# The end of an attention stage: places taken by halves, first output tiles half by half, weights two tiles ahead

## Chip, cores and metric

The kernel runs on one core of a Trainium2 chip. The metric is the device time of one execution in microseconds. The time before is the median of three executions, and one further execution was recorded by the profiler.

## The reference

The program is a two-layer trunk on a sequence of 1024 tokens with 1024 channels, all in float32: layer 0 is a gated linear attention with a convolutional feed-forward, layer 1 is a banded softmax attention with a convolutional feed-forward, and a final norm follows. The change lies in layer 1's attention and in the steps behind it. These are the parts that matter:

```python
CHUNK, B_HEADS, B_HEAD_DIM, LEFT_CHUNKS = 64, 16, 64, 8      # BAND = 9 * 64 keys

def rmsnorm(x, g):
    return x * lax.rsqrt(jnp.mean(x * x, axis=-1, keepdims=True) + EPS) * g

def chunk_attention(xn, w_q, rel_bias, w_out, k_pad, v_pad):
    q = (xn @ w_q).reshape(bsz, nc, CHUNK, B_HEADS, B_HEAD_DIM)...
    bias = rel_bias[:, clip(rel)]                   # one learned bias per head and distance
    def one_chunk(args):                            # 64 queries against 576 keys
        s = jnp.einsum("bqhd,bkhd->bhqk", q_n, k_band) * scale + bias
        s = jnp.where(valid, s, NEG_INF)
        p = jax.nn.softmax(s, axis=-1)
        return jnp.einsum("bhqk,bkhd->bqhd", p, v_band)
    o = lax.map(one_chunk, (jnp.arange(nc), q))
    return o.reshape(bsz, seq, B_WIDTH) @ w_out

# layer 1:
h = h + chunk_attention(rmsnorm(h, b_norm), w_q, rel_bias, w_out, k_pad, v_pad)
h = h + conv_ffn(rmsnorm(h, f_norm), ...)           # starts with xn @ w_up
```

## The kernel before

Activations lie with channels on the partitions: a matrix of 1024 channels and 1024 tokens is eight tiles of 128 channels, each in two halves of 512 tokens (`s` is the half, `k` the tile). Every float32 operand of a dense product is split into a high part (a cast on ScalarE, for activations and weights) and a low part (a subtraction on VectorE or GpSimd), and a product is three matmuls: high x high, high x low, low x high (`dense`, lines 120 to 122). One such triple on 512 columns is called a unit here.

Attention works on eight pairs of heads, `p` = 0 to 7. For each pair three tiles are projected (keys, queries, values; 16 units each, half 0 first). Beside them run the score blocks of an earlier pair: `score` (L2109 to L2125: matmuls, bias and row maximum on VectorE in one instruction, the negated maximum in a second one, exponential and row sum on ScalarE, reciprocal on VectorE, scaling on GpSimd), then transposes of the probabilities (`turn_run`, L2170), their split, and the product with the values (`apply_run`, L2215 and L2216), whose sum is written to `oT`. Finished pairs 0 to 5 are written to DRAM (`d_o`) and read back as the activations of the output projection.

The order of instructions on every engine is written by a planner (`Flow`) when the kernel is built. It keeps a planned time `T`, a cost for each engine's steps (`wv.on`), a list of short steps with ranks, and a queue of dense tiles, `wv.dense`. It takes a short step when one is due, and otherwise one unit of the dense queue. The engines then work through their instructions in that order and wait for each other's data on the chip. Of the dense tiles that follow the current one, the planner loads and splits weights ahead, with this function (`brief` is False in the kernel before):

```python
while len(self.nxt) < (2 if self.brief else 1):
    ...
    next(e[2])                                   # issues the load of the weights
    self.nxt.append([e[2], 1, self.T, e[1], 8])
if split and self.nxt and self.nxt[0][1] == 1 and (split > 1 or self.T >= self.nxt[0][2] + 6.0):
    self.nxt[0][1] = 2
    self.nxt[0][4] = next(self.nxt[0][0]) or 8   # the split; it gives the unit at which the next one may come
```

It is called from a tile's second unit on, with `split` true from the unit that the current tile has given. Where a tile's split has not come when the tile itself is due, it is put there.

The activations of the output projection lie in the places of the projection's inputs, `xh` and `xl`. They are taken (`act_tiles`) when the last value tile (pair 7) has been summed for both halves. From then on `early_o` casts the pairs 0 to 5 that were read back (L2263, low part L2266, odd tiles on GpSimd), and `own_act` the pairs 6 and 7 from `oT` (L340 and L341). `first_parts` computes the first output tiles over the six early pairs (`NO` = 6): tile 0 in both halves and tile 1 in half 0, advancing together with the pair `k` as the outer loop. `part` does tiles 2 to 7, `rest(0)` and `rest(1)` add pairs 6 and 7 of one half. `rest` also issues the steps of the norm in front of the feed-forward (`norm_steps`): squares, their sum, a matmul that sums over channels (`pss`, L372), square root, a matmul that broadcasts (`psb`, L385), product, cast and low part. Half 0 of that norm runs beside the remaining tiles of half 1, paced by `tail`; half 1 runs at the start of the feed-forward, whose first weights are `r` (L1439) and whose first matmuls are `pu` (L1393 to L1395).

Of the kernel before, what the change touches and what calls it, by code (L numbers as in the profile page):

```python
# [9 lines left out]
F32 = mybir.dt.float32  # L10
# [6 lines left out]
P = 128  # L17
# [11 lines left out]
def trunk_kernel(  # L29
# [94 lines left out]
    def hs(s):  # L124
        return slice(s * HALF, (s + 1) * HALF)
# [222 lines left out]
    env = {"acc": sum_in_acts}  # L348
    hp = wp = None

    def norm_steps(h, s, g, dst, keep=False):


        run = env["run"](s) if "run" in env else None
        acc = run if run is not None else env["acc"](s)
        before = None
        for k in range(KT):
            sq = acc if k == 0 else env["tmp"]()
            nc.scalar.activation(sq, h[k][:, hs(s)], AF.Square)
            if before is not None:  # L360
                nc.vector.tensor_tensor(acc, acc, before, op=ALU.add)
            before = sq if k > 0 else None
            yield
        if run is not None:
            acc = env["acc"](s)
            nc.vector.tensor_tensor(acc, run, before, op=ALU.add)
            yield
        else:
            nc.vector.tensor_tensor(acc, acc, before, op=ALU.add)
        pss = env["aux"]("pss")  # L370
        for t in range(4):
            mm(pss[:, 2 * t : 2 * t + 2], acc[:, t * P : (t + 1) * P], ones[:, 0:2], start=True, stop=True)  # L372
        rs = rsn[:, s]
        nc.scalar.activation(rs, pss[:, 0:8], AF.Sqrt, scale=1.0 / SEQ, bias=epst)
        nc.vector.reciprocal(rs, rs)
        yield
        act_tiles((s,), dst)

        def low(t_, k):
            eng = (nc.gpsimd if k < 4 else nc.vector) if keep and s == 1 else (nc.vector if k % 2 == 0 else nc.gpsimd)  # L380
            eng.tensor_tensor(dst[1][k][s], t_, dst[0][k][s].bitcast(F32), op=ALU.subtract)  # L381

        psb = env["aux"]("psb")
        for t in range(4):
            mm(psb[:, t * P : (t + 1) * P], rs[:, 2 * t : 2 * t + 1].broadcast_to([P, P]), ident, start=True, stop=True)  # L385
        before = None
        for k in range(KT):
            t_ = h[k][:, hs(s)] if keep else env["tmp"]()
            if g is None:
                nc.vector.tensor_tensor(t_, psb[:, 0:HALF], h[k][:, hs(s)], op=ALU.mult)  # L390
            else:
                nc.vector.scalar_tensor_tensor(t_, h[k][:, hs(s)], g[:, k : k + 1], psb[:, 0:HALF], op0=ALU.mult, op1=ALU.mult)
            nc.scalar.copy(dst[0][k][s], t_)
            if before is not None:
                low(*before)
            before = t_, k
            yield
        low(*before)
# [1554 lines left out]
    with ExitStack() as ph:  # L1953
# [37 lines left out]
        def queue_kv(p):  # L1991
# [56 lines left out]
            def post_v(s, ps):  # L2048
                if s == 0:
                    kv["v"] = [(odd if p % 2 else even).tile([P, 8, P], F32R, name="V", tag="V", bufs=2) for _ in range(2)]  # L2050
                vt = bp.tile([P, HALF], F32, name="vt", tag="vt", bufs=3)
                nc.scalar.copy(vt, ps)
                t0 = wv.on("A", 0.6)
                wv.add(0.7, "turn", lambda: t0 - wv.slack, turn(s, vt))
                if (p, s) == (7, 1):
                    act_tiles((0, 1), acts)
                    wv.mark("acts")

            if p == 0:
                pss = next(first)  # L2060
# [36 lines left out]
        def score(u, kv, a, t, bt):  # L2097

            nk = min(t, 4) + 1
            W = nk * P  # L2100
            ps = pB.tile([P, 2, HALF], F32, name="sc", tag="sc", bufs=1)
            n = 2 if nk > 4 else 1
            w = W // n
            k0 = (t - nk + 1) * P
            qs = slice(t * P, (t + 1) * P)
            kA, qA, qL = kv["k"], kv["q"], kv["ql"]
            for i in range(n):
                c = slice(k0 + i * w, k0 + (i + 1) * w)
                mm(ps[:, i, 0:w], qA[a][:, qs], kA[a][:, c], start=True, stop=False)  # L2109
                mm(ps[:, i, 0:w], qL[a][:, qs], kA[a][:, c], start=False, stop=True)  # L2110
            wv.pe(2 * n, max(0.11, w * 0.45e-3))
            S = bp.tile([P, n, w], F32, name="sS", tag="sS", bufs=6)
            st = bp.tile([P, 4], F32, name="st", tag="st", bufs=8)
            nc.vector.tensor_tensor_reduce(out=S, in0=ps[:, 0:n, 0:w], in1=bt[:, 0:W][:, ::-1].rearrange("p (n w) -> p n w", n=n), op0=ALU.add, op1=ALU.max, scale=1.0, scalar=3.0 * NEG, accum_out=st[:, 0:1])  # L2114
            nc.vector.tensor_scalar(st[:, 1:2], st[:, 0:1], -1.0, None, op0=ALU.mult)
            sc_free[0] = t0 = wv.on("D", 0.35 + 1.04e-3 * W)

            def power():
                nc.scalar.activation(S, S, AF.Exp, bias=st[:, 1:2], accum_out=st[:, 2:3])
                wv.later(wv.on("A", 0.45 + 0.75e-3 * W), share)  # L2120

            def share():
                nc.vector.reciprocal(st[:, 3:4], st[:, 2:3])  # L2123
                t_ = wv.on("D", 0.13)
                nc.gpsimd.tensor_scalar(S, S, st[:, 3:4], 1.0, op0=ALU.mult, op1=ALU.mult)  # L2125
                wv.mark(u, wv.on("G", 0.2 + 1.04e-3 * W, t_))

            wv.later(t0, power)
            return S.rearrange("p n w -> p (n w)"), t - nk + 1

# [101 lines left out]

        def close(p, a, tp, oT, t):
            if p == 7 and a == 1 and tp % 2 == 1:
                wv.add(1, ("own", tp // 2), wv.when("acts"), own_act(oT, tp // 2, 7))
            if p < 7 and (a, tp) == (1, 3):
                if p == 6:
                    for s in range(2):
                        wv.add(1, ("own", s), wv.when("acts"), own_act(oT, s, 6))
                wv.mark(("o", p), t)  # L2240
                if p < 6:
                    wv.later(t + 5.0, lambda: (nc.sync.dma_start(out=d_o[p], in_=oT), wv.mark(("d_o", p), wv.T + 4.0)))
# [15 lines left out]
        def early_o(k, s):  # L2258
            yt = bp.tile([P, HALF], F32, name="yo", tag="yo", bufs=6)
            nc.sync.dma_start(out=yt, in_=d_o[k][:, hs(s)])  # L2260
            yield wv.T + 3.0
            yield from wait("acts")
            nc.scalar.copy(acts[0][k][s], yt)  # L2263
            t = wv.on("A", 0.65)
            yield t - wv.slack
            (nc.vector if k % 2 == 0 else nc.gpsimd).tensor_tensor(acts[1][k][s], yt, acts[0][k][s].bitcast(F32), op=ALU.subtract)  # L2266
            wv.mark(("act", k, s), wv.on("D", 0.7) if k % 2 == 0 else wv.on("G", 1.4, t))
# [23 lines left out]
            wv.on("G", 2.1, wv.on("A", 0.8))  # L2291
            return wt

        def part_end(m, s, ps):
            if m not in loaded:
                loaded.add(m)
                nc.sync.dma_start(out=h[m], in_=d_h[m])
            nc.vector.tensor_tensor(h[m][:, hs(s)], ps, h[m][:, hs(s)], op=ALU.add)
            wv.on("D", 0.7)

# [2 lines left out]
        def first_parts():  # L2303
# [2 lines left out]
            wts = [part_split(raws[0])]  # L2306
            yield 20
            wts.append(part_split(raws[1]))
            jobs = [(wts[m], m, s, pacc.tile([P, HALF], F32, name="acco", tag="acc", bufs=3)) for m, s in ((0, 0), (0, 1), (1, 0))]
            for k in range(NO):  # L2310
                for n, (wt, m, s, ps) in enumerate(jobs):
                    if (k, n) != (0, 0):
                        yield there(("act", k, s), *([("begun")] if (k, n) == (NO - 1, 2) else []))
                    dense(ps, wt, 0, *acts, FULL[k : k + 1], s, first=k == 0, last=k == NO - 1)
            for wt, m, s, ps in jobs:
                part_end(m, s, ps)
            yield
            yield from part_units(wts[1], 1, 1)

# [8 lines left out]

        def part(m, halves):
            raw = part_raw(m)  # L2330
            yield
            wt = part_split(raw)
            yield 3 if len(halves) == 1 else None
            for s in halves:
                yield from part_units(wt, m, s)

# [2 lines left out]
        def rest(s):  # L2339
# [10 lines left out]
            for m in range(KT):  # L2350
# [11 lines left out]
                def then(s=s, m=m):  # L2362
                    nc.scalar.dma_start(out=quarter(d_r1, m, s), in_=h[m][:, hs(s)])
                    if m == 0:
                        its[s] = norm_steps(h, s, g_f[:, 1], normed, keep=True)
                    next(its[s])
                    wv.on("D", 0.75, wv.on("A", 0.65))
                    if m == KT - 1:
# [6 lines left out]
                yield  # L2375

        def tail(it):
            for _ in it:
                yield wv.T + 1.2

        queue_kv(0)
        wv.auto = False
# [4 lines left out]
        with tc.manual_schedule():  # L2387
# [2 lines left out]
            wv.add(1, "score", lambda: 0.0, score_run())  # L2390
            wv.add(0.8, "turns", lambda: 0.0, turn_run())
            wv.add(0.6, "apply", lambda: 0.0, apply_run())
            for n, (k, s) in enumerate([(k, s) for k in range(NO) for s in range(2)]):
                wv.add(0.9, ("early", n % 6), wv.when(("d_o", k)), early_o(k, s))
            wv.add(0, "begin", wv.when(("o", 6), ("act", 6, 0), ("act", 6, 1)), begin())
            wv.dense.append((lambda: True, there(("act", 0, 0)), first_parts()))
# [104 lines left out]
```

## Time and profile before

| what | us |
|---|---|
| median of three runs | 2595.81 |
| lowest and highest of them | 2591.06, 2598.98 |
| the profiled execution, its own time | 2593.14 |
| its span in the profile | 2591.4 |
| first and last score block on VectorE (start) | 1371.0, 1822.9 |
| first matmul of the output projection (start) | 1782.2 |
| first matmul of the layer's feed-forward (start) | 1910.2 |

Times inside the profile count from the start of the span. PE is TensorE's matmul, PEld its weight load, DVE is VectorE, ACT ScalarE, POOL GpSimd, and SP the queue that issues most loads. In a row of the timeline stand start, length, engine, line, operation, what it writes from what it reads, the shape, the count, and in brackets the idle time in front of it and what ended it.

### The profile page before, as it was taken

Reading aid. Unit: us, or ns where it says so; the run is one execution under the profiler, and the core shown is the slowest. Engines: PE = TensorE matmul, PEld = TensorE weight load, DVE = VectorE, ACT = ScalarE, POOL = GpSimd, SP = SyncE. Lnnn points to the kernel's source line nnn. Section 1 sums busy time; section 2 is a strip of 40 time slices with the busy share of each in tenths; the row PEclk is TensorE's granted clock in tenths of the full one; section 3 lists DMA queues with packets and bytes.
Section 4 is the critical chain, followed back from the end, with each engine's and each line's share of the span. In section 5 each row is a group of like instructions: output and inputs, shape, how many; then the busy total and the mean of one; then the engine's idle time right before and its main releaser. Section 6 shows DMA issues by size and latency. Waiting matters only on the chain. (4 is left out here: it accounts for less than half of the span.)

```text
span 2591.4 us, 39359 instructions
## 1 busy us (share of the span) xinstructions
PE 2513.5 (97%) x13933; PEld 2078.2 (80%) x13933; DVE 1856.7 (72%) x3102; ACT 1410.0 (54%) x2708; POOL 1494.1 (58%) x1517
## 2 busy tenths in 40 slices
PE   7999999999999999999999999999999999999998
PEld 5878888888777888888778888887876788888877
DVE  5765775454588888888876666666478788888875
ACT  6444555464455656565455556655345556565543
POOL 3655554345447777777735444444443777777771
PEclk9999999999999999999999999999999999999999
DMA  4534345455336777777841111212332577777785
GB/s 128 138 99 121 116 117 164 134 178 169 96 85 143 146 148 154 153 145 153 186 145 48 47 52 57 73 37 73 133 104 78 134 150 143 154 154 153 154 194 175
DMA packets 317061, 325.93 MB, mean 126 GB/s; under 512 B 32832, under 2 KB 240960, under 8 KB 316864
## 3 DMA queue, kind: packets, MB, share of 16 engines
q1 hardware_dynamic: 285728, 219.33, 28.6%
q0 software_dynamic: 26240, 95.43, 20.6%
q10 hardware_dynamic: 4896, 8.65, 0.9%
q8 instruction: 110, 1.80, 0.3%
q14 instruction: 87, 0.71, 0.1%
HBM read 180.68 MB, written 142.67 MB: 125 GB/s over the span
## 5 line engine op out<-in xcount | busy, mean ns | idle before, releaser
L1360 POOL TENSOR_TENSOR ul<-r,uh 128x512 fp32r<-128x512 f32 x282 | 445.6, 1599 | 295.2 <-ACT uh L1381 273.9
L120 PE MATMUL acc<-xh,whi 128*128 128x512 f32 x896 | 375.5, 420 | 0.3 <-ACT xh L1099 0.2
L105 POOL TENSOR_TENSOR wlo<-wraw,whi 128x256 fp32r<-128x256 f32 (+3 forms) x338 | 248.8, 767 | 206.0 <-ACT whi L103 178.1
L122 PE MATMUL acc<-xh,wlo 128*128 128x512 f32 x896 | 353.3, 394 | 4.2 <-POOL wlo L105 4.2
L121 PE MATMUL acc<-xl,whi 128*128 128x512 f32 x896 | 353.4, 394 | 1.3 <-DVE xl L1100 0.8
L1381 ACT CAST uh<-r 128x512 fp32r<-128x512 f32 x296 | 181.7, 623 | 219.8 <-DVE r L1360 175.2
L1395 PE MATMUL pu<-xh,ul 128*128 128x512 f32 x552 | 217.3, 394 | 3.3 <-POOL ul L1360 3.2
L1393 PE MATMUL pu<-xh,uh 128*128 128x512 f32 x552 | 216.7, 393 | 2.9 <-ACT uh L1381 1.4
L1394 PE MATMUL pu<-xl,uh 128*128 128x512 f32 x552 | 216.3, 392 | 1.0 <-POOL xl L381 1.0
L2125 POOL TENSOR_SCALAR sS<-sS,st 128x640 f32<-128x640 f32 (+4 forms) x128 | 86.4, 680 | 206.5 <-DVE st L2123 197.6
L122 PEld LDWEIGHTS acc<-xh,wlo 128*128 128x128 f32 x896 | 168.8, 188 | 42.6 <-POOL wlo L105 5.3
L1714 ACT COPY stage<-pd 128x1024 f32<-128x1024 f32 x180 | 174.8, 1013 | 49.4 <-PE pd L1395 49.4
L121 PEld LDWEIGHTS acc<-xl,whi 128*128 128x128 f32 x896 | 170.0, 190 | 27.8 <-DVE xl L1100 3.1
L120 PEld LDWEIGHTS acc<-xh,whi 128*128 128x128 f32 x896 | 169.7, 189 | 24.5 <-ACT xh L1099 1.2
L1488 DVE SCALAR_TENSOR_TENSOR val<-vpre,colt,val 128x1023 f32<-128x1023 f32 (+2 forms) x92 | 153.6, 1670 | 38.6 <-ACT val L1485 38.4
L2114 DVE CUSTOM_DVE_ANT_0 sS<-sc,bt 128x640 f32<-128x640 f32 (+4 forms) x128 | 84.1, 657 | 132.5 <-PE sc L2110 87.1
L1360 POOL TENSOR_TENSOR dl<-a,dh 128x512 fp32r<-128x512 f32 x90 | 154.8, 1720 | 38.4 <-ACT dh L1381 38.4
L1488 DVE SCALAR_TENSOR_TENSOR gate<-gpre,colt,gate 128x1023 f32<-128x1023 f32 (+2 forms) x92 | 175.4, 1906 | 0.8
L1360 DVE TENSOR_TENSOR r<-r,r 128x512 f32<-128x512 f32 x168 | 131.6, 783 | 31.1 <-POOL ul L1360 29.7
L1395 PEld LDWEIGHTS pu<-xh,ul 128*128 128x128 f32 x552 | 104.3, 189 | 28.0 <-POOL ul L1360 6.6
L1393 PEld LDWEIGHTS pu<-xh,uh 128*128 128x128 f32 x552 | 104.3, 189 | 25.3 <-ACT uh L1381 1.8
L2183 ACT CAST pTh<-ptp 128x512 fp32r<-128x512 f32 (+2 forms) x176 | 75.4, 452 | 89.7 <-PE ptp L2170 86.3
(390 smaller groups left out, 7125.9 us busy)
## 6 DMA issues: line engine op xcount, KB each, us to landing
r<-in_f_w_up_dram SPq DMA_DIRECT2D x172, 256.0 KB, 4.2
d_r<-stage POOLq DMA_DIRECT2D x78, 512.0 KB, 7.9
d_c<-stage POOLq DMA_DIRECT2D x70, 512.0 KB, 7.9
a<-in_f_w_down_dram SPq DMA_DIRECT2D x72, 256.0 KB, 2.8
wraw<-in_a_w_in_dram SPq DMA_DIRECT2D x32, 512.0 KB, 4.7
d_e<-stage POOLq DMA_DIRECT2D x32, 512.0 KB, 9.1
wraw<-in_a_w_out_dram SPq DMA_DIRECT2D x16, 512.0 KB, 4.3
d_r<-h ACTq DMA_DIRECT2D x32, 256.0 KB, 3.6
```

Source lines behind the costliest of these rows:

```text
L105: nc.gpsimd.tensor_tensor(lo[:, c], raw[:, c], hi[:, c].bitcast(F32), op=ALU.subtract)
L120: mm(ps, hi[:, kw, wcol : wcol + P], rh[k][s], start=st, stop=False)
L121: mm(ps, hi[:, kw, wcol : wcol + P], rl[k][s], start=False, stop=False)
L122: mm(ps, lo[:, kw, wcol : wcol + P], rh[k][s], start=False, stop=sp)
L1360: tt = lambda eng, o, a, b, op: eng.tensor_tensor(o, a, b, op=op)
L1381: copy(hi, src)
L1393: mm(ps, w[0][:, cw], x[0], start=first, stop=False, skip_group_check=True)
L1394: mm(ps, w[0][:, cw], x[1], start=False, stop=False, skip_group_check=True)
L1395: mm(ps, w[1][:, cw], x[0], start=False, stop=last, skip_group_check=True)
L1488: nc.vector.scalar_tensor_tensor(t_[:, a:c1], p_[:, a - step : c1 - step], w[:, 2 - step : 3 - step], t_[:, a:c1], op0=ALU.mult, op1=ALU.add)
L1714: nc.scalar.copy(t_, ps)
L2125: nc.gpsimd.tensor_scalar(S, S, st[:, 3:4], 1.0, op0=ALU.mult, op1=ALU.mult)
```

## The change

The places of the output projection's activations are taken one half at a time, each when the last value tile has been summed for that half. The steps that read pairs 0 to 5 back are listed with all of half 0 first. `first_parts` runs three pairs of tile 0 in half 0, then tile 1 and tile 0 in half 0 in turn, and then tile 0 in half 1; the sums of half 0 are added to `h` at the third unit of half 1. From there on two tiles are loaded ahead (`brief`), and each tile gives an earlier unit for the next one's split. `h[m]` is loaded beside a tile's weights, if its place exists by then. The norm's last sum of squares becomes a step of its own in half 0, with new distances between the steps in `tail`. Scores are kept negated: the instruction on VectorE that adds the bias multiplies by -1 and takes the minimum, the exponential multiplies by -1, and the instruction that negated the maximum is gone; the planner's cost of a block falls from 0.35 to 0.2 plus the same part per column.

```diff
@@ norm_steps
-    def norm_steps(h, s, g, dst, keep=False):
+    def norm_steps(h, s, g, dst, keep=False, gap=False):
...
             nc.vector.tensor_tensor(acc, acc, before, op=ALU.add)
+            if gap:
+                yield
         pss = env["aux"]("pss")
@@ post_v
-                if (p, s) == (7, 1):
-                    act_tiles((0, 1), acts)
-                    wv.mark("acts")
+                if p == 7:
+                    act_tiles((s,), acts)
+                    wv.mark(("acts", s))
@@ score
-            nc.vector.tensor_tensor_reduce(..., op0=ALU.add, op1=ALU.max, scale=1.0, scalar=3.0 * NEG, accum_out=st[:, 0:1])
-            nc.vector.tensor_scalar(st[:, 1:2], st[:, 0:1], -1.0, None, op0=ALU.mult)
-            sc_free[0] = t0 = wv.on("D", 0.35 + 1.04e-3 * W)
+            nc.vector.tensor_tensor_reduce(..., op0=ALU.add, op1=ALU.min, scale=-1.0, scalar=-3.0 * NEG, accum_out=st[:, 0:1])
+            sc_free[0] = t0 = wv.on("D", 0.2 + 1.04e-3 * W)
...
-                nc.scalar.activation(S, S, AF.Exp, bias=st[:, 1:2], accum_out=st[:, 2:3])
+                nc.scalar.activation(S, S, AF.Exp, scale=-1.0, bias=st[:, 0:1], accum_out=st[:, 2:3])
@@ close and early_o: wait for ("acts", half) in place of "acts"
...
@@ part_end
+        def load_h(m):
+            if h and m not in loaded:
                 loaded.add(m)
                 nc.sync.dma_start(out=h[m], in_=d_h[m])
+
+        def part_end(m, s, ps):
+            load_h(m)
             nc.vector.tensor_tensor(h[m][:, hs(s)], ps, h[m][:, hs(s)], op=ALU.add)
@@ first_parts
             wts.append(part_split(raws[1]))
-            jobs = [(wts[m], m, s, pacc.tile(...)) for m, s in ((0, 0), (0, 1), (1, 0))]
-            for k in range(NO):
-                for n, (wt, m, s, ps) in enumerate(jobs):
-                    if (k, n) != (0, 0):
-                        yield there(("act", k, s), *([("begun")] if (k, n) == (NO - 1, 2) else []))
-                    dense(ps, wt, 0, *acts, FULL[k : k + 1], s, first=k == 0, last=k == NO - 1)
-            for wt, m, s, ps in jobs:
-                part_end(m, s, ps)
+            wv.brief = True
+            order = [(0, 0, k) for k in range(3)]
+            for k in range(3, NO):
+                order += [(1, 0, k - 3), (0, 0, k)]
+            order += [(1, 0, k) for k in range(NO - 3, NO)] + [(0, 1, k) for k in range(NO)]
+            banks, done = {}, []
+            for n, (m, s, k) in enumerate(order):
+                if n > 0:
+                    yield there(("act", k, s), *(["begun"] if (m, s, k) == (0, 1, 2) else []))
+                if (m, s, k) == (0, 1, 2):
+                    for i in range(2):
+                        part_end(i, 0, banks[i, 0])
+                if k == 0:
+                    banks[m, s] = pacc.tile([P, HALF], F32, name="acco", tag="acc", bufs=3)
+                dense(banks[m, s], wts[m], 0, *acts, FULL[k : k + 1], s, first=k == 0, last=k == NO - 1)
+            part_end(0, 1, banks[0, 1])
@@ part
             raw = part_raw(m)
+            load_h(m)
             yield
             wt = part_split(raw)
-            yield 3 if len(halves) == 1 else None
+            yield 1 if len(halves) == 1 else 3
@@ rest and tail
-                        its[s] = norm_steps(h, s, g_f[:, 1], normed, keep=True)
+                        its[s] = norm_steps(h, s, g_f[:, 1], normed, keep=True, gap=s == 0)
...
-            for _ in it:
-                yield wv.T + 1.2
+            for n, _ in enumerate(it):
+                yield wv.T + (0.8, 2.2)[n] if n < 2 else wv.T + 1.1
@@ the list of steps
-            for n, (k, s) in enumerate([(k, s) for k in range(NO) for s in range(2)]):
+            for n, (s, k) in enumerate([(s, k) for s in range(2) for k in range(NO)]):
                 wv.add(0.9, ("early", n % 6), wv.when(("d_o", k)), early_o(k, s))
```

More of the change, by code (lines that the diff above doesn't have):

```diff
@@ L2113, in score @@
             st = bp.tile([P, 4], F32, name="st", tag="st", bufs=8)
-            nc.vector.tensor_tensor_reduce(out=S, in0=ps[:, 0:n, 0:w], in1=bt[:, 0:W][:, ::-1].rearrange("p (n w) -> p n w", n=n), op0=ALU.add, op1=ALU.max, scale=1.0, scalar=3.0 * NEG, accum_out=st[:, 0:1])
-            nc.vector.tensor_scalar(st[:, 1:2], st[:, 0:1], -1.0, None, op0=ALU.mult)
-            sc_free[0] = t0 = wv.on("D", 0.35 + 1.04e-3 * W)
+            nc.vector.tensor_tensor_reduce(out=S, in0=ps[:, 0:n, 0:w], in1=bt[:, 0:W][:, ::-1].rearrange("p (n w) -> p n w", n=n), op0=ALU.add, op1=ALU.min, scale=-1.0, scalar=-3.0 * NEG, accum_out=st[:, 0:1])
+            sc_free[0] = t0 = wv.on("D", 0.2 + 1.04e-3 * W)
             def power():
-                nc.scalar.activation(S, S, AF.Exp, bias=st[:, 1:2], accum_out=st[:, 2:3])
+                nc.scalar.activation(S, S, AF.Exp, scale=-1.0, bias=st[:, 0:1], accum_out=st[:, 2:3])
                 wv.later(wv.on("A", 0.45 + 0.75e-3 * W), share)
@@ L2234, in close @@
             if p == 7 and a == 1 and tp % 2 == 1:
-                wv.add(1, ("own", tp // 2), wv.when("acts"), own_act(oT, tp // 2, 7))
+                wv.add(1, ("own", tp // 2), wv.when(("acts", tp // 2)), own_act(oT, tp // 2, 7))
             if p < 7 and (a, tp) == (1, 3):
@@ L2238, in close @@
                     for s in range(2):
-                        wv.add(1, ("own", s), wv.when("acts"), own_act(oT, s, 6))
+                        wv.add(1, ("own", s), wv.when(("acts", s)), own_act(oT, s, 6))
                 wv.mark(("o", p), t)
@@ L2261, in early_o @@
             yield wv.T + 3.0
-            yield from wait("acts")
+            yield from wait(("acts", s))
             nc.scalar.copy(acts[0][k][s], yt)
@@ L2292, in part_split @@
             return wt
-        def part_end(m, s, ps):
-            if m not in loaded:
+        def load_h(m):
+            if h and m not in loaded:
                 loaded.add(m)
                 nc.sync.dma_start(out=h[m], in_=d_h[m])
+        def part_end(m, s, ps):
+            load_h(m)
             nc.vector.tensor_tensor(h[m][:, hs(s)], ps, h[m][:, hs(s)], op=ALU.add)
@@ L2308, in first_parts @@
             wts.append(part_split(raws[1]))
-            jobs = [(wts[m], m, s, pacc.tile([P, HALF], F32, name="acco", tag="acc", bufs=3)) for m, s in ((0, 0), (0, 1), (1, 0))]
-            for k in range(NO):
-                for n, (wt, m, s, ps) in enumerate(jobs):
-                    if (k, n) != (0, 0):
-                        yield there(("act", k, s), *([("begun")] if (k, n) == (NO - 1, 2) else []))
-                    dense(ps, wt, 0, *acts, FULL[k : k + 1], s, first=k == 0, last=k == NO - 1)
-            for wt, m, s, ps in jobs:
-                part_end(m, s, ps)
+            wv.brief = True
[14 more added lines that the diff above has]
+            part_end(0, 1, banks[0, 1])
             yield
```

## The prediction, written before the result was known

> **What bounds the kernel now.** I read the page first, then the windows around the changed lines, then the list of TensorE's waits in them, then each engine's timeline at the places of the longest waits.
>
> ```profile
> span 2591.4 us, 39359 instructions
> PE 2513.5 (97%) x13933; PEld 2078.2 (80%) x13933; DVE 1856.7 (72%) x3102; ACT 1410.0 (54%) x2708; POOL 1494.1 (58%) x1517
> ```
>
> TensorE is the bound nearly everywhere. So an edit pays only where TensorE waits or where its clock is below full speed. The windows show where that is (columns: stretch, length, busy time of PE, PEld, DVE, ACT, POOL, then granted clock, DMA share, GB/s).
>
> ```profile
> 1370.00:1780.00 410.00, 408.04 (x2384) 355.74 (x2385) 261.63 (x793) 240.29 (x569) 193.45 (x320) 1.00 0.18 51
> 1780.00:1804.00 24.00, 19.33 (x77) 14.92 (x75) 12.78 (x37) 14.27 (x35) 14.74 (x15) 0.79 0.51 165
> 1788.00:1792.00 4.00, 4.00 (x13) 3.29 (x12) 2.43 (x8) 1.73 (x4) 2.82 (x4) 0.50 0.88 277
> 1895.00:1904.00 9.00, 7.13 (x23) 4.91 (x22) 4.78 (x7) 3.50 (x5) 6.73 (x5) 0.81 0.19 71
> 1904.00:1916.00 12.00, 11.85 (x53) 9.44 (x51) 11.69 (x15) 6.20 (x11) 8.12 (x7) 1.00 0.83 268
> ```
>
> The 410 us of attention proper (heads, projections) hold 2 us without TensorE work, at clock 1.00. Nothing is to be had there. The loss is in the handover to the output projection, 1780 to 1804, and again at 1895 to 1904. Busy time hides the second half of it: at 1788 to 1792 TensorE is busy 4.00 of 4.00 at half clock. The clock costs 24.00 x 0.21 = 5.04 us in the first place and 9.00 x 0.19 = 1.71 us in the second. To that come TensorE's waits from 1780 to 1932 (total, times, longest):
>
> ```profile
> PE acco L120 <- ACT whi L103: 5.3, 4, 2.7
> PE acco L121 <- POOL xl L2266: 1.9, 2, 1.6
> PE acco L122 <- POOL wlo L105: 1.3, 2, 0.7
> PE pss L372 <- DVE nacc L369: 1.3, 2, 0.9
> PE acco L120 <- DVE h L2298: 1.0, 2, 0.8
> ```
>
> All the room is therefore 5.04 + 1.71 + 5.3 + 1.9 + 1.3 + 1.0 + 0.9 (the first of the two pss waits; the other is in the next half, which the change leaves as it is) = 17.15 us, 0.66% of the run. No reading of this change gains more, unless the plan of the 410 us changes too.
>
> **First output tiles half by half, places taken by halves.** What happens there now:
>
> ```profile
> 1766.43 0.58 ACT L2052 COPY vt<-acc 128x512 f32<-128x512 f32 x1 [1.98 <-PE acc L122]
> ...
> 1778.19 0.59 ACT L2052 COPY vt<-acc 128x512 f32<-128x512 f32 x1 [0.86 <-PE acc L122]
> ...
> 1780.08 3.21 ACT L2263 CAST xh<-yo 128x512 fp32r<-128x512 f32 x6
> ...
> 1785.72 0.84 ACT L103 CAST whi<-wraw 128x768 fp32r<-128x768 f32 x1
> ```
>
> ```profile
> 1786.61 0.79 PE L120 MATMUL acco<-xh,whi 128*128 128x512 f32 x1 [2.73 <-ACT whi L103]
> 1798.44 0.50 PE L121 MATMUL acco<-xl,whi 128*128 128x512 f32 x1 [1.64 <-POOL xl L2266]
> ```
>
> ```profile
> 1794.98 2.18 POOL L2125 TENSOR_SCALAR sS<-sS,st 128x384 f32<-128x384 f32 x2 [2.96 <-DVE st L2123]
> 1797.13 2.50 POOL L2266 TENSOR_TENSOR xl<-yo,xh 128x512 fp32r<-128x512 f32 x2
> ```
>
> The last projection ends for half 0 at 1766.4 and for half 1 at 1778.2 (the two vt copies). Places are taken only after the second, so twelve casts and twelve subtractions come at once, and ACT reaches the weights of tile 1 (1785.72) behind six casts of 3.21 us. TensorE waits 2.73 us, and later 1.64 + 0.3 for the low parts on GpSimd. With places by halves the six casts of half 0 and their subtractions can run from 1766.4, beside 12 us of projection matmuls. The first tiles then start on ready data. They need nothing of half 1 for 12 units (three matmuls each; rows 1910.21 and 1910.89 below give 0.68 us), so 8.2 us plus the attention work between them. In that time GpSimd must do three subtractions at 1.25 (3.8 us), and tile 1's weights are wanted only from the fourth unit, 2 us in. Because half 0 is already marked, nothing holds the first unit back, so the split of tile 1 is put into ACT's queue ahead of the casts of half 1; that is the point where I choose. Room: 2.73 + 1.9 of waits and 5.04 of clock, 9.7. I leave 1.0 for a short wait at tile 1 and its clock: **gain 8.7**, ends 0 and 9.7.
>
> The clock part rests on the clock falling because of these waits. The trace has 0.50 right behind a wait of 2.73, a fall behind 1.64, and 1.00 through the 410 us without such a wait. The Trainium skill, "TensorE: Matmul & The Clock Gate", section "Part 1: The HAM clock gate", has the array go to half clock after an idle window of about 3.4 us. By that rule neither wait is long enough, and the 5.04 us would not go with the waits; here the row decides, and what is left if it doesn't is a rival below.
>
> What the earlier casts cost: they go into ACT's queue ahead of exponentials (L2119) and casts of probabilities (L2183), six at once, 3.21 us, for which transposes and the probability-value matmuls wait. The nearest row is in the same stretch, the only wait that TensorE has there regularly:
>
> ```profile
> PE pvt L2033 <- ACT vt L2052: 1.4, 7, 0.2
> ```
>
> Ends: nothing (the projection's eight units of half 1, 5.4 us, cover 3.21) and 3.21 plus as much clock as in the 1780 window, about 3.5 (5.04/4.63 of it), so 6.7. A gain is excluded, since there is no wait to remove. I take a **loss of 0.5**, near the pvt row, because the projection units cover it; without them it is 3.21. The DMAs of half 1 (L2260) move too; each waits on SP for a low part to free its buffer. SP's row now:
>
> ```profile
> 1782.42 4.31 SPq L2260 DMA_DIRECT2D yo<-d_o  x4
> ```
>
> Behind it on SP stand the weights of tiles 2 and 3. They are needed some 18 units later, so nothing is charged.
>
> The sums of the first two tiles of half 0 are now added four matmul units before their banks are wanted, and h is loaded when the weights are, not at the add. That removes the 1.0 of the h row: **gain 1.0**. DVE's long wait for a late h (below) goes with it; it has cost TensorE 0.2 of that 1.0.
>
> ```profile
> 1865.52 0.69 DVE L2298 TENSOR_TENSOR h<-acco,h 128x512 f32<-128x512 f32 x1 [5.53 <-DMA h<-d_h]
> ```
>
> **Weights two tiles ahead.** The planner puts a tile's split no sooner than 6 us of planned time after its load. A one-half tile is only 4.1 us long, so with one tile ahead the split came at the tile's own start:
>
> ```profile
> 1849.57 0.37 ACT L2221 COPY tm<-poT 64x256 f32<-64x256 f32 x1 [5.91 <-PE poT L2216]
> 1849.84 0.83 ACT L103 CAST whi<-wraw 128x768 fp32r<-128x768 f32 x1
> ```
>
> ```profile
> 1850.73 0.50 PE L120 MATMUL acco<-xh,whi 128*128 128x512 f32 x1 [1.19 <-ACT whi L103]
> ...
> 1880.40 1.05 PE L372 MATMUL pss<-ones,nacc 128*128 128x2 f32 x8 [0.90 <-DVE nacc L369]
> ...
> 1895.85 0.50 PE L120 MATMUL acco<-xh,whi 128*128 128x512 f32 x1 [0.53 <-ACT whi L103]
> ...
> 1898.89 0.79 PE L122 MATMUL acco<-xh,wlo 128*128 128x512 f32 x1 [0.72 <-POOL wlo L105]
> ```
>
> The cast stood behind a copy that waited for attention's last matmul. Two ahead, it can come a tile earlier. The whi waits without the first are 5.3 - 2.73 = 2.6; I take **2.3**, ends 0 and 2.6. The wait of the norm's sum (0.90) goes when the add has its own step 0.8 us ahead: **gain 0.9**; what is late next there is the square root's chain, which already lies under matmuls.
>
> The last stage of the projection (1895.85 on) has 1.3 for wlo and 1.71 of clock, 3.0. Here I expect most to come back. Its end is met by the next layer's first weights:
>
> ```profile
> 1902.78 0.37 SPq L1439 DMA_DIRECT2D r<-in_f_w_up_dram  x1
> ...
> 1906.91 1.08 POOL L1381 CAST uh<-r 128x512 fp32r<-128x512 f32 x1
> 1908.07 1.81 POOL L1360 TENSOR_TENSOR ul<-r,uh 128x512 fp32r<-128x512 f32 x1
> ...
> 1910.21 0.39 PE L1393 MATMUL pu<-xh,uh 128*128 128x512 f32 x1
> ...
> 1910.89 0.39 PE L1393 MATMUL pu<-xh,uh 128*128 128x512 f32 x1
> ```
>
> The low part ul is ready at 1909.88 and is used with the third matmul, 1910.67: 0.8 us of slack. The load follows the first tile of this stage, so the 1.3 of wlo pulls it along, the clock does not. VectorE, busy 11.69 of 12.00 at 1904 to 1916 (fourth stretch above), won't go faster either, and the next norm sum stands at its end. **Gain 1.0**, ends 0 and 3.0.
>
> **Negated scores.** One instruction less per score block:
>
> ```profile
> L2115 DVE TENSOR_SCALAR st<-st x128: 153/154/157, 1371.4 to 1823.7; 128x1 f32<-128x1 f32 x128
> ```
>
> 128 x 0.154 = 19.7 us of VectorE, which is busy 261.63 of 410: off the path. Min in place of max and a factor of -1 are taken at the same 0.75 us; no row shows them. The planner's cost per block falls by 0.15, as does the real one, so order and chip move together. Value 0; ends: a gain of 1.4 (the pvt row), a loss of 1.4 if each such wait doubles.
>
> **Sum.** 8.7 - 0.5 + 1.0 + 2.3 + 0.9 + 1.0 = 13.4 us. The profiled run took 2593.14 (span 2591.4 and 1.74 around it), so 2579.7; the median 2595.81 lies 2.67 above that run, so **2582.4**. With the ends for the unknown costs the gain runs from 9 to 17: 2578.8 to 2586.8.
>
> **Rivals.** (A) The bursts only move: six casts in attention's stream cost 3.21 and clock (6.7 in all in place of 0.5). For: ACT runs its queue in order, and the row at 1780.08 shows that six go out together. Against: projection units are in reserve. Gain 7.2: 2588.6. Half the weights' gain lost beside it gives 2590.
>
> (B) The clock is low there for another reason and stays: 4.5 of the 8.7 is lost, gain 8.9, 2586.9. Against: it falls only behind waits. The rule of the Trainium skill's page on TensorE, cited above, points this way.
>
> (C) The change doesn't do what it says: casts of both halves still come together, for instance if the buffers of half 1's loads or the weights of tile 1 still come last, and the first tiles keep their 9.7. Gain 13.4 - 8.2 = 5.2: 2590.6.
>
> (D) Slower: the new cost of a score block shifts the written order of TensorE in all seven repeated head pairs, and a score or transpose is placed ahead of what it needs. Price: one wait like that of 1786.61 with its clock, 2.73 + 2.97 = 5.7 us per pair, 40 for seven, so 2595.8 + 40 - 13.4 = 2622. It decides from three such pairs (17 against 13.4); four are needed for 0.3%. For: TensorE waits 0.2 at the same place in each of seven pairs, so the order is tight. Against: the real block shortens by what the plan's does, and VectorE has a third of its time free.
>
> **How the numbers follow.** Main case 0.60, A 0.21, B 0.04, C 0.07, D 0.08. What a measurement of this kernel can tell from no change is about 0.3%, 7.8 us: below 2588.0 is faster, above 2603.6 slower. Faster: nearly all of the main case, a quarter of A, two thirds of B: 0.66. Slower: most of D: 0.07. Same: 0.27. The range goes from 2576 (all the room and 3 us of the runs' own spread, 2591 to 2599) to 2595, which takes in A, B and C and leaves out D and little else. The likeliest case alone: 2579 to 2587.
>
> **What would show it.** Right: the 1780 window at clock near 1.00, no whi wait of over 1 us at the first tiles, casts of half 0 between 1766 and 1778, no pss wait in half 0, and a new wait of one or two us at the first pu matmuls or the second pss. Wrong: a clock below 0.9 at the handover, TensorE waits on ptp, pTh or sc between 1766 and 1800, or a wait that returns with each head pair before 1766, which would be D.

## The result and the profile after

The changed kernel takes 2579.11 us (median of six), the kernel before 2595.15 beside it: ratio 0.9941, 95% interval 0.9929 to 0.9953, 16.0 us faster. A second measurement with five rounds gave 2579.72 against 2591.07, ratio 0.9952 (0.9938 to 0.9965), 11.4 us. The forecast was 13.4 us, a ratio of 0.9948.

Times of whole runs scatter by some us even for one kernel. The two profiled executions of the changed kernel (2574.87 and 2579.72) differ ahead of the attention: its first copy starts at 1373.49 in one and at 1378.75 in the other, and up to there 5.2 and 10.2 us went to the clock (length times one minus the granted clock, over windows of 4 us). So I compare stretches inside the profiles: from the first pair's value copy (half 0, L2052, L2054 after) to the last pair's, called attention, and from there to the first feed-forward matmul that reads the low part `ul`, called handover. Before they are 390.7 and 144.2 us, after 389.4 and 130.8: 14.7 us less together. The second profile of the changed kernel gave 389.4 and 130.8 again, so this measure repeats to 0.1.

The two copies that bound attention, in the timeline of ScalarE of the changed kernel:

```profile
1373.49 0.59 ACT L2054 COPY vt<-acc 128x512 f32<-128x512 f32 x1 [0.80 <-ACT sS L2120]
...
1762.91 0.59 ACT L2054 COPY vt<-acc 128x512 f32<-128x512 f32 x1 [0.28 <-PE acc L122]
```

The windows of the changed kernel (columns as before the change):

```profile
1766.00:1780.00 14.00, 12.09 (x69) 10.15 (x68) 8.59 (x19) 10.76 (x25) 11.58 (x16) 1.00 0.46 142
1780.00:1804.00 24.00, 23.11 (x129) 19.47 (x128) 15.81 (x44) 11.98 (x32) 10.05 (x13) 1.00 0.32 109
1850.00:1895.00 45.00, 41.65 (x187) 33.40 (x187) 32.16 (x46) 21.48 (x34) 28.08 (x30) 1.00 0.54 171
```

The clock is 1.00 all through; before, 5.04 and 1.71 us went to it (6.8 over the whole handover, in finer windows). TensorE's waits from 1766 to 1920 in the changed kernel:

```profile
PE acco L122 <- POOL wlo L105: 2.7, 3, 1.9
PE pu L1395 <- POOL uh L1383: 1.4, 1, 1.4
PE pu L1397 <- POOL ul L1362: 1.1, 1, 1.1
PE pu L1396 <- POOL xl L383: 1.0, 2, 0.7
PE sc L2111 <- DVE st L2116: 0.8, 1, 0.8
```

No wait for whi, for the low parts of the projection's activations, for h or for the first half's norm sum is left. New are 1.9 at the first output tiles, 1.4 + 1.1 at the first feed-forward matmuls and 0.8 for a score block at 1789. The 1.0 for `xl` is not new: the kernel before has the same wait (L1394 for L381, 1.0 in two times), which the prediction's list leaves out. In the handover the listed waits fall from 10.6 to 6.0 us and the clock's loss from 6.8 to nothing, 11.4 of its 13.4; the other 2.0 are not resolved. How the wait of 1.9 comes about, on GpSimd and on ScalarE:

```profile
1768.42 2.44 POOL L105 TENSOR_TENSOR wlo<-wraw,whi 128x128 fp32r<-128x128 f32 x4 [11.94 <-issue]
1770.85 0.36 POOL L2126 TENSOR_SCALAR sS<-sS,st 128x128 f32<-128x128 f32 x1
1771.19 3.79 POOL L2267 TENSOR_TENSOR xl<-yo,xh 128x512 fp32r<-128x512 f32 x3
1774.97 1.43 POOL L2126 TENSOR_SCALAR sS<-sS,st 128x256 f32<-128x256 f32 x1
1776.37 2.71 POOL L105 TENSOR_TENSOR wlo<-wraw,whi 128x128 fp32r<-128x128 f32 x4
```

```profile
1764.31 3.23 ACT L2264 CAST xh<-yo 128x512 fp32r<-128x512 f32 x6
1767.43 0.84 ACT L103 CAST whi<-wraw 128x768 fp32r<-128x768 f32 x1
...
1772.53 0.84 ACT L103 CAST whi<-wraw 128x768 fp32r<-128x768 f32 x1
1773.27 1.66 ACT L2264 CAST xh<-yo 128x512 fp32r<-128x512 f32 x3
```

The high part of tile 1's weights does stand ahead of the casts of half 1 (1772.53 against 1773.27). But its low part (1776.37) stands on GpSimd behind tile 0's low part and the three subtractions of half 0.

### The profile page after: what moved, and what is told of

It reads as the page before. It is cut to its first block, busy times and chain, and to the rows that moved or that the text cites. A ratio compares the mean times of both kernels' runs of the same rounds, so it can differ in the third digit from the quotient of the medians.

```text
span 2572.9 us, 39308 instructions
## 1 busy us (share of the span) xinstructions
PE 2499.4 (97%) x13933; PEld 2071.4 (81%) x13933; DVE 1841.5 (72%) x2974; ACT 1407.6 (55%) x2708; POOL 1498.7 (58%) x1517
## 5 line engine op out<-in xcount | busy, mean ns | idle before, releaser
L1396 PEld LDWEIGHTS pu<-xl,uh 128*128 128x128 f32 x552 | 103.9, 188 | 23.4 <-POOL xl L383 2.1
```

Source lines behind the costliest of these rows:

```text
L1396: mm(ps, w[0][:, cw], x[1], start=False, stop=False, skip_group_check=True)
```

## Experiments

Stretches in us; ratio and interval against the kernel before in the same measurement, where there were five rounds. Two columns split the handover: `waits` is the sum of TensorE's listed waits in it, `clock` what it loses to a granted clock below 1.00 (length times one minus the clock, over windows of 2 us).

| kernel | attention | handover | waits | clock | sum | ratio |
|---|---|---|---|---|---|---|
| before | 390.7 | 144.2 | 10.6 | 6.8 | 534.9 | |
| after | 389.4 | 130.8 | 6.0 | 0 | 520.2 | 0.9941 (0.9929 to 0.9953) |
| e1 scores only | 389.4 | 140.5 | 11.9 | 1.7 | 529.9 | 0.9995 (0.9986 to 1.0004) |
| e2 all but scores | 390.7 | 130.9 | 4.7 | 0 | 521.6 | 0.9960 (0.9946 to 0.9973) |
| e3 halves only | 390.7 | 133.9 | 4.7 | 1.7 | 524.6 | 0.9967 (0.9956 to 0.9978) |
| e4 not two ahead | 389.4 | 132.3 | 7.2 | 0 | 521.7 | 0.9959 (0.9947 to 0.9971) |
| e5 places together | 389.3 | 130.8 | 5.8 | 0 | 520.2 | 0.9956 (0.9942 to 0.9969) |
| e6 no gap | 389.4 | 131.3 | 6.1 | 0 | 520.7 | one run |
| e7 plan's cost only | 389.4 | 140.4 | 11.8 | 1.7 | 529.8 | one run |
| e8 chip's part only | 389.7 | 142.0 | 11.1 | 3.4 | 531.7 | one run |
| e9 places only | 390.7 | 140.1 | 9.5 | 3.4 | 530.8 | one run |
| e10 after again | 389.4 | 130.8 | 6.0 | 0 | 520.2 | 0.9952 (0.9938 to 0.9965) |
| e11 six first | 389.4 | 128.6 | 4.1 | 0 | 518.0 | 0.9943 (0.9930 to 0.9955) |
| e12 six first, cast on ScalarE | 389.4 | 130.2 | 5.7 | 0.5 | 519.6 | 0.9956 (0.9943 to 0.9968) |

**Scores alone (e1), and all but the scores (e2).** e1 is the kernel before with the `score` hunks of the change, e2 the changed kernel with them taken back.

> The kernel before with the negated scores alone (instruction, exponential and the planner's cost of 0.2). Theory, that the handover's waits and clock make 11 to 12 of the 16 us and the shorter score block only tightens the written order of the head pairs: 2 to 4 us faster than before (ratio 0.9985 to 0.9992), the stretch 1780 to 1804 still with a clock below 0.85 and a wait of over 2 us for whi. Rival, that the 19.7 us which VectorE no longer works carry the gain: 8 us or more faster (ratio 0.997 or less).

> The changed kernel with the scores as before (two instructions, planner's cost 0.35). Theory: 12 to 14 us faster than before (ratio 0.9946 to 0.9954), clock at the handover 1.00, the head pairs 56.8 us apart as before instead of 56.4. Rival, that the scores carry the gain: 8 us faster at most.

The scores alone give 5.0 us inside the profile, more than the 2 to 4 expected, and their whole-run ratio can't be told from 1. Added to the rest they give 1.4 (521.6 to 520.2); e2 itself is 13.3 under the kernel before, in its band. Of e1's 5.0, 3.7 lie in the handover. It waits no less there than the kernel before (11.9 against 10.6), but loses 1.7 us to the clock instead of 6.8; the clock of 0.93 at 1780 to 1804 and a longest wait for whi of 1.2 are not the signs that the theory named. The changed kernel loses nothing to the clock in the handover, with these scores or without (e2). So the scores don't carry the gain, and of the freed 19.7 us of VectorE at most 1.4 is in it.

**The first tiles by halves alone (e3).**

```diff
 (the changed kernel, with)
-            wv.brief = True
-            load_h(m)                                  # in part
-            yield 1 if len(halves) == 1 else 3
+            yield 3 if len(halves) == 1 else None
 (scores and norm steps as before)
```

> The kernel before with the places taken by halves, the steps that read pairs back listed by halves, and the first tiles half by half; one tile ahead, splits at the old units, h loaded at the add, norm sum and scores as before. Theory: 8 to 10 us faster than before (ratio 0.9961 to 0.9969): handover at clock 1.00 with one wait of about 2 us, while the waits for whi at the later tiles (1.19, 0.85, 0.53) and for the norm's sum (0.90) stay. Rival, that the weights two tiles ahead are what frees the handover: 3 us faster or less, and a whi wait of over 2 us at the first tiles.

10.3 us less than before, a little over the band, without two tiles ahead: 5.9 of waits and 5.1 of clock, less 0.7 elsewhere. The wait of about 2 us that I expected at the first tiles isn't there (0.42 for wlo). TensorE's longest waits show that the first tiles are free and the later ones stay, and behind the wait for the norm's sum the clock fell once (1.7 us):

```profile
PE acco L122 <- POOL wlo L105: 1.9, 4, 0.7
PE acco L120 <- ACT whi L103: 1.4, 2, 0.8
PE pss L374 <- DVE nacc L369: 0.9, 1, 0.9
```

**One tile ahead (e4).** The changed kernel without `brief` and with the old split units.

> The changed kernel with one tile ahead and the old units for the splits; everything else as changed. Theory: 2 to 3 us slower than the changed kernel, so 13 to 14 us faster than before (ratio 0.9946 to 0.9950), with the waits for whi at later tiles back. Rival, that two tiles ahead carry the gain: within 8 us of the kernel before.

1.5 us more than the changed kernel: one whi wait of 1.2 is back. That is less than the 2 to 3 expected, and no more than a fraction of the gain.

**Places together (e5) and places only (e9).**

```diff
 (e5: the changed kernel, with)
-                if p == 7:
-                    act_tiles((s,), acts)
-                    wv.mark(("acts", s))
+                if (p, s) == (7, 1):
+                    act_tiles((0, 1), acts)
+                    for i in range(2):
+                        wv.mark(("acts", i))
```

e9 is the kernel before with the opposite edit: places and marks by halves, the order of steps and first tiles as before.

> The changed kernel with the places of both halves taken together, after the last projection; order of steps and tiles by halves as changed. Theory, that the early places are what lets the casts of half 0 run beside the last projection: 5 to 9 us slower than the changed kernel (ratio to before 0.996 to 0.9975), all casts behind 1770, a wait of 2 us or more at the first output tiles and mostly a clock below 0.9 behind it. Rival, that the order by halves is enough: within 2 us of the changed kernel, clock 1.00.

> The kernel before with the places taken by halves and nothing else; the steps that read pairs back are listed pair by pair and the first tiles advance in both halves together, as before. From the last value tile's half 0 (its copy on ScalarE) to the first feed-forward matmul the kernel before takes 143.8 us, the changed one 129.0. Theory after the run with both places taken together, that the order of the first tiles by halves is what counts: 139 to 145 us, with the wait for the first tiles' weights or low parts still above 1.5 us. Rival, the prediction's own step, that the early places are what frees the handover: 135 or less.

This felled the step that I thought carried the gain. With the places taken together the sum is 520.2, the changed kernel's to 0.1, although the casts of half 0 come only after the last projection:

```profile
1778.75 3.23 ACT L2265 CAST xh<-yo 128x512 fp32r<-128x512 f32 x6
```

The planner then puts attention work into the time of the casts, and the first output unit starts 7.3 us later, counted from the first copy; that work has to be done somewhere. The equal sum is made of unequal parts, though. e5 doesn't have the wait of 1.9 for tile 1's low part, and has others in its place (0.9 for `xl`, 0.6 for `oT`). Early places with the old order take 139.6 us by the measure of the expectation, in the theory's band, and give 4.1 us. Long waits stay (whi 2.6, low part 2.1):

```profile
PE acco L120 <- ACT whi L103: 4.0, 3, 2.6
PE acco L121 <- POOL xl L2266: 2.1, 1, 2.1
```

Of the 4.1, 3.4 is clock. That much less clock was lost in e8 too, which takes the places as before, so it can't be credited to the places; the waits fell by 1.1, from 10.6 to 9.5. So the order by halves frees the handover: with it, and the places late, the waits are 5.8 and the clock's loss nothing. None of the nine profiles with that order has a fall of the clock at the first output tiles; each of the five without it has one or two. Early places are worth about 1 us of waits without it, and nothing in the order of the changed kernel. What they are worth in e11's order, where the wait of 1.9 is gone, was not tried. Nor was the order in which pairs are read back tried apart from the order of the first tiles.

**Norm sum in one step with its add (e6).** `gap` off and all steps 1.2 apart.

> The changed kernel without the norm sum's own step and with 1.2 between all steps of the norm. From the first score matmul to the first feed-forward matmul the changed kernel takes 523.7 us. Theory: 0.5 to 1.5 us longer, with a wait for the norm's sum of about 0.9 in half 0. Rival: no longer, since the first feed-forward weights end the stage anyway.

525.6 from the first score to the first feed-forward matmul, 1.9 more and above the band, but the waits at that matmul (2.5) are gone in exchange; counted to the low part's matmul it is 0.5. The theory's wait returned (0.70 for the sum), and with it two for whi that it hadn't named (0.82 and 0.54). The rival is right on most of the time: the feed-forward's weights end the stage.

**Plan or chip (e7, e8).** e7 changes only `0.35` to `0.2`; e8 has the new instructions and keeps 0.35.

> The kernel before with the planner's cost of a score block at 0.2 in place of 0.35 and nothing else. From the first score matmul to the first feed-forward matmul the kernel before takes 539.7 us, and with the negated scores and this cost together 534.7. Theory, that the written order makes those 5 us: 533 to 537, pairs 56.4 us apart. Rival, that the shorter block on VectorE makes them: 539 or more.

> The kernel before with the negated scores and the planner's cost left at 0.35, so the order on every engine stays as written. Theory, that the order makes the 5 us: 538.5 to 540.5 us from the first score matmul to the first feed-forward matmul, pairs 56.8 apart. Rival, that the shorter block makes them: 537 or less, and shorter pairs.

e7 took 534.6 and does what e1 does, so the plan is enough. But e8 took 536.5, below its band: attention got 1.0 shorter without any change of order, nearly as much as with the new plan (1.3), and both together give 1.3. So either loosens the pairs, and neither theory is right alone. The instruction itself costs the same in both forms; its rows in the kernel before and in the changed one:

```profile
L2114 DVE CUSTOM_DVE_ANT_0 sS<-sc,bt x128: 291/753/827, 1371.0 to 1822.9; 128x640 f32<-128x640 f32 x64, 128x128 f32<-128x128 f32 x16, 128x256 f32<-128x256 f32 x16, 128x384 f32<-128x384 f32 x16
```

```profile
L2116 DVE CUSTOM_DVE_ANT_0 sS<-sc,bt x128: 272/754/827, 1368.8 to 1815.1; 128x640 f32<-128x640 f32 x64, 128x128 f32<-128x128 f32 x16, 128x256 f32<-128x256 f32 x16, 128x384 f32<-128x384 f32 x16
```

The other 2.2 us of e8 lie in the handover, where its waits are as long as before (whi 5.5 in all, xl 2.6), but 3.4 us go to the clock instead of 6.8. Nothing in e8 orders the handover differently, so half of that loss of the kernel before doesn't follow from its order and its waits alone; the last section shows on what else it depends.

**The changed kernel again, and two versions that go on (e10, e11, e12).** e11 and e12:

```diff
-            order = [(0, 0, k) for k in range(3)]
-            ...
+            order = [(m, 0, k) for m in range(2) for k in range(NO)] + [(0, 1, k) for k in range(NO)]
 (e12 also)
-            ... nc.gpsimd.tensor_copy if r == 0 else nc.scalar.copy)
+            ... nc.gpsimd.tensor_copy if r == 0 and (layer, c) != (1, 0) else nc.scalar.copy)
```

> The changed kernel once more, for a second profile and for times beside the next two. Theory: the same waits within 0.2 us at the same places (129 to 131 us of handover), while the clock behind them need not fall the same. Rival, that the clock follows the length of the waits: 1.00 everywhere again.

> The changed kernel with all six pairs of tile 0 in half 0 ahead of tile 1, so that the low part of tile 1's weights, which now comes 1.91 us late behind three subtractions on GpSimd, has three units (2 us) and the attention work among them more. Theory: that wait gone and 1.5 to 2 us faster than the changed kernel. Rival, that the wait only goes on to the next late thing (scores, half 1's low parts): within 0.7 us.

> As the run before, and the high part of layer 1's first feed-forward weights is cast on ScalarE (0.6 us there) instead of GpSimd (1.1 to 1.2, behind a subtraction of 1.6). Theory: the waits at the first feed-forward matmuls fall from 1.4 + 1.1 to 1.5 to 2 in all, 0.5 to 1 us faster than with six first alone. Rival: the low part still ends it on GpSimd and nothing is gained.

e10 doesn't decide between its two expectations in the handover: 130.8 us, the same waits, and the clock at 1.00 again. Ahead of the attention the same kernel lost 10.2 us to the clock where its first profile lost 5.2.

e11 is 2.2 us shorter in the profile than the changed kernel, a little more than expected, and the wait of 1.9 is gone; its median, 2575.72, is the lowest of all, 4.0 under e10 beside it, though the intervals overlap. It is the version to keep. e12 lost 1.6 of that again, which neither of its expectations had: in ScalarE's queue the cast stands behind the norm's squares, so the wait for it grew from 1.4 to 3.3.

```profile
1891.67 0.50 PE L1395 MATMUL pu<-xh,uh 128*128 128x512 f32 x1 [1.40 <-POOL uh L1383]
1893.53 0.50 PE L1397 MATMUL pu<-xh,ul 128*128 128x512 f32 x1 [1.12 <-POOL ul L1362]
```

```profile
1898.67 0.50 PE L1395 MATMUL pu<-xh,uh 128*128 128x512 f32 x1 [3.30 <-ACT uh L1383]
1900.23 0.80 PE L1397 MATMUL pu<-xh,ul 128*128 128x512 f32 x1 [0.82 <-POOL ul L1362]
```

(Above e11, below e12.)

## Why the prediction held, step by step

**The room and where it lies** held in the main: of the room of 17.15 us, the clock's 6.8 went and 4.6 of the waits. The handover as a whole gave 13.4, and attention, where I saw nothing to be had, gave 1.3.

**First tiles: 8.7 + 1.0 for h - 0.5 for the burst, 9.2 in all; e3 measured 10.3**, clock included (e3 leaves the h loads at the add). The size was right, the reason half wrong. I put it on casts that run beside the last projection; e5 shows that these are not needed. What counts is that the first units ask for half 0 only, so half as many casts and subtractions stand in front of them. That half as many stand there is read from the queues, not tried by itself. The burst that I charged with 0.5 cost at most 0.3, a wait for `ptp` in e2 and e3 that the kernel before lacks.

**The clock**: I priced it in proportion to the waits (2.97 for 2.73). It doesn't come so: each fall took 1.7 us or twice that, and e4, with nearly the waits of the changed kernel, had one just behind the stretch that I measure. The whole 6.8 went because the waits that are left didn't set off a fall, and the last section shows that this was partly luck.

**Tile 1's weights**: I argued from ScalarE's queue and was right there, but didn't follow the same tile's low part through GpSimd's queue. It waited 1.91, where I had left 1.0 with the clock; e11 took the wait away and got 2.2. In e2 and e3, with the scores as before, the same matmul waits 0.42, so the wait needs the order written for the new scores as well.

**Two tiles ahead**: 2.3 forecast, 1.5 measured (e4). **Norm sum**: 0.9 forecast, 0.5 (e6), since what is late next is the feed-forward's weights, not the square root.

**The last stage of the projection** was mis-sized: forecast a gain of 1.0 with ends 0 and 3.0, measured a loss of 0.9. From its first matmul to the low part's first use it took 1895.85 to 1910.67, 14.8 us; after it takes 15.8:

```profile
1877.99 0.39 PE L120 MATMUL acco<-xh,whi 128*128 128x512 f32 x1
...
1891.88 0.50 PE L1395 MATMUL pu<-xh,uh 128*128 128x512 f32 x1 [1.41 <-POOL uh L1383]
...
1893.74 0.50 PE L1397 MATMUL pu<-xh,ul 128*128 128x512 f32 x1 [1.12 <-POOL ul L1362]
```

The mechanism was the one named, the next layer's first weights, with a new wait of the size that I gave as its sign. What I missed is that the work of the norm's first half is not shortened by a faster projection and now falls into this stage: a subtraction for it, which itself waits 3.30 us for ScalarE, holds GpSimd until the weights' cast can start.

```profile
1889.09 1.63 POOL L383 TENSOR_TENSOR xl<-h,xh 128x512 fp32r<-128x512 f32 x1 [3.30 <-ACT xh L395]
1890.65 1.17 POOL L1383 CAST uh<-r 128x512 fp32r<-128x512 f32 x1
```

VectorE was as full as I took it to be: 11.69 of 12.00 us before (1904 to 1916), and after:

```profile
1884.00:1896.00 12.00, 9.46 (x41) 7.22 (x40) 11.69 (x17) 6.21 (x11) 8.23 (x7) 1.00 0.80 246
```

**Scores**: 0 forecast with ends of 1.4 either way; 1.4 measured, at the end.

**The sum**: 14.7 us in the stretches against the 13.4 forecast is partly luck. The first tiles and the scores gave 2.5 more than forecast; the last stage, two tiles ahead and the norm's sum gave 3.1 less. The parts as measured add up to 12.8 only, since each was tried against a different kernel.

**The rivals.** A (the bursts only move) and C (no effect at the first tiles) are out by the clock of 1.00 and by e3. One sign that I gave for being wrong did show, a wait of 0.77 on `sc` at 1789.12; e2 and e3 don't have it, so it belongs to the new scores. B (the clock stays low for another reason) is out as a whole, but it had a grain: e8 keeps the waits and loses half as much clock. D (slower through the plan in each pair) is out: the plan's shift makes attention shorter (390.7 to 389.4).

## What to carry to other kernels

When a stage begins with many small preparations, let the first products ask for half of the data first; taking the places earlier may add little. Follow a moved tile through every queue that prepares it, not only the first: the longest new wait came from the second. When a stage is shortened, look for work of other engines that is not shortened with it, and charge it at the stage's end.

## What the runs showed of the hardware

The clock's fall is not fixed by the wait in front of it. The changed kernel waited 1.91 at the first tiles and 1.4 + 1.1 at the feed-forward with the clock at 1.00 after all of them. In the handovers of all these profiles each fall goes to 0.50 and lasts 3.4 us or twice that, so it costs 1.7 us or 3.4. The falls of the kernel before in the handover:

```profile
1785.89:1792.72 6.83, 6.11 (x17) 5.05 (x18) 3.15 (x9) 4.55 (x9) 4.20 (x6) 0.50 0.83 261
1799.55:1802.96 3.41, 3.27 (x10) 2.68 (x11) 0.00 (x0) 0.04 (x1) 3.33 (x4) 0.50 0.01 2
1898.53:1901.94 3.41, 3.05 (x7) 2.47 (x8) 0.69 (x1) 1.18 (x2) 3.08 (x4) 0.50 0.19 73
```

Their starts lie on a grid: 13.66 and 112.64 us behind the first, 4 and 33 steps of 3.413. All nine falls of that execution from 311.3 to 2526.6 fit the same grid to 0.1 us (read in windows of 0.1 us). That suggests that it counts how much of a step TensorE is idle, and a wait can lie in one step or be cut in two. e4 and e10 have the same waits at the feed-forward, 1.4 and 1.1, at nearly the same time, and the clock fell in one and not in the other. In e4 nearly all of both lies in one step (TensorE busy 1.03 of 3.41), and in e10 they lie in two (e4 above, e10 below):

```profile
1895.70:1899.11 3.41, 1.03 (x3) 0.59 (x4) 3.31 (x5) 1.84 (x3) 3.33 (x4) 1.00 0.88 268
1899.11:1902.52 3.41, 3.41 (x9) 2.64 (x8) 2.69 (x3) 0.93 (x2) 3.33 (x3) 0.50 1.00 298
```

```profile
1894.22:1897.63 3.41, 1.97 (x9) 1.15 (x7) 3.41 (x6) 2.31 (x5) 3.25 (x3) 1.00 0.85 234
1897.63:1901.04 3.41, 2.29 (x10) 1.75 (x10) 3.10 (x4) 1.25 (x2) 3.33 (x3) 1.00 0.96 323
```

In the handovers of all the profiles, nine steps at full clock had TensorE busy for less than 1.5 us, and a fall followed each. Of seven with 1.6 to 1.9 three were followed by one, and of those with more a single one (2.51, in e3). The changed kernel's two emptiest steps had 1.62 and 1.80.

That agrees with the window that runs freely, in the section of the Trainium skill which the prediction cites ("TensorE: Matmul & The Clock Gate", "Part 1: The HAM clock gate"), though a whole window of idle time of about 3.4 us, as it has it, was not needed here. In planning, a wait of one to three us should be charged with 1.7 us of clock as a chance, not with a sum in proportion to it.

The first weights of the feed-forward were held on SP until a write of `h` from ScalarE's queue had landed (in the trace, SP's load waits 11.9 us in three waits for `d_r`). Why a load should wait for that write was not tried and stays open.
